# Attention values of a decoder's second layer: full float32 with two heads in the two column halves, in place of split float32 with zero blocks

## The chip, the cores and the metric

The kernel runs on one core of a Trainium2 chip. The metric is the device time of one execution in microseconds (us), taken as the median of several runs. The core has five engines: PE (matmuls; the profile lists its weight loads apart, as PEld), DVE (vector), ACT (scalar), POOL and SP (here it issues the transfers). PE writes its results to PSUM, and DVE and ACT read them from there.

## The reference, cut to what matters

Two decoder layers work on 512 tokens of width 1024. Layer 0 mixes with a gated delta rule beside an attention into 256 memory tokens. Layer 1 mixes with a sliding-window attention of 12 heads (width 64, two shared key/value heads, a sink logit for each head) beside a memory attention of 4 heads. Each mixer is followed by a layer norm, an MLP with a hidden width of 4096, and a layer norm. The change is in the attention of layer 1, of which this is the part that counts:

```python
def mixer_b(h, mem, k_sh, v_sh, cos, sin, w_in, sinks, mem_w_kv, w_o):
    proj = h @ w_in
    q = apply_rope(proj[..., :SWA_Q_W].reshape(B, S, SWA_HEADS, SWA_DH), cos, sin)
    o = sliding_window_sink_attention(q, k_sh, v_sh, sinks)   # o = probs @ values of 2 blocks of 128 keys
    mo = memory_cross_attention(proj[..., SWA_Q_W:], mem, mem_w_kv)   # mo = probs @ 256 memory values
    return jnp.concatenate([o, mo], axis=-1) @ w_o
```

## The kernel before

All arithmetic stands for float32. Most matmuls are done in a faster format on split operands: a number is cut into a high part (ACT casts it) and a low part (DVE subtracts), and three matmuls, high by high, high by low and low by high, make one product. `split_copy` (L117) makes the pair, `token_major` (L106) and `feature_major` (L98) are the products with weights, and `wload` (L81) loads a slab of weights and splits it. A matmul on plain float32 operands stands in the trace as two matmul records.

Layer 1's mixer runs over 4 tiles of 128 tokens (t). `shared_kv` (L1051) makes a tile's rotated keys and its values; `projq` (L1068) makes half of a tile's queries (tile `projqMM`, transposes `projqpt`); `attend` (L1083) pushes two units for each half of a tile, and each unit holds four heads in two pairs (j), with r naming a pair's two heads. In the second half of a tile the second unit is the memory attention (`mem`). So there are 16 units: 12 of the sliding window, 3 of which see one block of keys (t = 0) and 9 two blocks, and 4 of the memory.

A unit has three parts. `scores` (L1097, tile `ssc`) multiplies 64-row operands: the two heads of a pair lie in the two halves of the array's rows, and the softmax follows on DVE (mask and maximum, L1119; scaling, L1137) and ACT (exponential, L1126). `turn` (L1139) transposes the probabilities on PE (tile `spt`, L1145) and copies them out of PSUM. `values` (L1154) multiplies by the values into the tile `ov` and splits the result into `XH`/`XL` or `mixTs`, from which `out1` (L1178) takes it for the output product (`wo`).

In `values` both heads of a pair are summed into one result of 128 rows: head 0 in rows 0 to 63, head 1 in rows 64 to 127. To do that with the array's whole width, the values stand with a block of 64 zeros between the two value heads (`vSs`, `VM1`, L1048 and L1025), and each matmul takes a 128-column slice, values and zeros or zeros and values. Window units work on split probabilities (`pTh`, `pTl`) and split values (`vSh`, `vSl`): 12 matmuls of 256 columns for two blocks, 6 for one. Memory units work in plain float32: 8 matmuls of 128 columns.

`push` (L584) interleaves the units: the scores of the newest, the turn of the one before, the values of the one before that. The order of the steps is the string `LAYER1_ORDER` (L40), run by `run_steps` (L44). On this order the framework's scheduler sets each engine's final order; every engine then works strictly in that order. PSUM tiles rotate: three for the large products (`mm`), five for the small ones (`sm`), and a product waits until the tile three places back has been read.

Of the kernel before, what the change touches and what calls it, by code (L numbers as in the profile page):

```python
# [18 lines left out]
P = 128  # L19
# [30 lines left out]
def trunk(ctx: ExitStack, tc: tile.TileContext, xT, xn, memT, wk, wq, wv, wqm, wz, wmk, wmv, wo0, wo1, up, dn,  # L50
# [533 lines left out]
    def push(unit):  # L584

        unit[0]()
        pend.append(unit)
        if len(pend) > 1:
            pend[-2][1]()
        if len(pend) > 2:  # L590
            pend.pop(0)[2]()
# [428 lines left out]
    with tc.tile_pool(name="l1", bufs=2) as lp:  # L1020
# [3 lines left out]

        KMr, VM1 = lt([P, 2, 256], "pm", 2), lt([P, 2, 2, 3, 64], "VM1", 1)  # L1025
        V.memset(VM1[:, :, :, 1, :], 0.0)
# [3 lines left out]
        for b in range(2):  # L1030
            for j in range(2):
                SY.dma_start(VM1[:, b, j, 0::2, :], kv1[1, :, b * 256 + j * P:b * 256 + (j + 1) * P].rearrange(
                    "p (r d) -> p r d", r=2))
# [14 lines left out]
        vSs = [lt([P, NT, 3, 64], n, 1, F32R) for n in ("vSh", "vSl")]  # L1048
        for v in vSs:
            V.tensor_scalar(v[:, :, 1, :], band[:, :].rearrange("p (t d) -> p t d", t=NT), 0.0, None, op0=ALU.mult)  # L1050
        def shared_kv(t):  # L1051
            ps = mmt("ropeMM")
            token_major(ps[:, :256], slabs["S"], x_tok(XH, t), x_tok(XL, t))
            split_copy(ps[:, P:2 * P].rearrange("p (g d) -> p g d", g=2), *[v[:, t, 0::2, :] for v in vSs])
# [28 lines left out]
        def attend(half, t):  # L1083
# [6 lines left out]
            def unit(q):  # L1090
# [48 lines left out]
                def turn():  # L1139
                    st["pT"] = []  # L1140
                    for r in range(2):
# [4 lines left out]
                        if mem:  # L1146
                            pT = fr(lt([P, 2, 2, P], "pTh", 4, F32R))
                            A.copy(pT, pt)
                        else:
                            pT = [lt([P, 2, 2, P], n, 4, F32R) for n in ("pTh", "pTl")]  # L1150
                            split_copy(pt[:, :nk], *[x[:, :nk] for x in pT])
                        st["pT"].append(pT)

                def values():  # L1154
                    pT = st["pT"]
                    ov = smt("ov")[:, 0:256].rearrange("p (j i) -> p j i", j=2)
                    if mem:
                        for j in range(2):
                            for i in range(4):
                                T.matmul(ov[:, j, :], VM1[:, i % 2, j, i // 2:i // 2 + 2, :].rearrange("p a d -> p (a d)"),  # L1160
                                         pT[i // 2][:, i % 2, j, :], start=(i == 0), stop=(i == 3))
                    else:
                        for r in range(2):
                            ph, pl = pT[r]
                            for b in range(nb):
                                vh, vl = (v[:, t - nb + 1 + b, r:r + 2, :].rearrange("p a d -> p (a d)") for v in vSs)
# [108 lines left out]
```

## Time and profile before

| what | value |
|---|---|
| median of 3 runs | 1191.41 us (1190.02 to 1192.32) |
| the profiled execution's own time | 1191.65 us |
| span of its trace | 1189.9 us |
| granted PE clock, mean | 0.991 |
| PE, DVE, ACT busy, share of the span | 97%, 73%, 48% |
| bytes moved by the transfers | 114.17 MB, 96 GB/s on average |

The profile is of one execution. A row of the trace names the line, the engine, the operation and the tiles (result <- operands); times are in us unless marked ns. In a shape such as 64*128 64x256 the first pair is the part of the array, rows by columns, and the second the operand that is streamed, 64 rows by 256 columns here. Matmul records are pipelined: a record lasts longer than the distance to the next one, so costs are read from start to start. Layer 1's attention lies between about 675 and 810 us of the span.

### The profile page before, as it was taken

The page shows a single profiled execution, that of the slowest core. Times are in us where ns is not written, and L with a number is a line of the kernel's source. Part 1 is how long each engine was busy: PE and PEld are TensorE (multiplying, and loading weights), DVE is VectorE, ACT ScalarE, POOL GpSimd, SP SyncE. Part 2 cuts the span into 40 slices and gives each one's busy share as a digit, 9 for nine tenths or more (in the row PEclk, how much of TensorE's full clock was granted, in tenths as well). Part 3 has the DMA queues.
Part 4 walks back from the last instruction along what each step waited for, and adds up shares of the span by engine and source line. Part 5 has one row for each costly group of instructions (what it writes and reads, how often), then busy time and mean ns, then how long its engine had stood idle before and what let it go on. Part 6 is the DMA issues. An engine that isn't in the chain of part 4 may idle for free.

```text
span 1189.9 us, 19072 instructions
## 1 busy us (share of the span) xinstructions
PE 1158.1 (97%) x7512; PEld 1025.7 (86%) x7512; DVE 866.3 (73%) x1621; ACT 566.3 (48%) x1024; POOL 229.0 (19%) x180
## 2 busy tenths in 40 slices
PE   9899999999999999999999999999999999999996
PEld 8877788879998898998988888788989998989985
DVE  5478889777798666666656968886986666666657
ACT  5345454655484443545443346662653534445341
POOL 0112111101014413232220100000042314232204
PEclk9899999999999999999999999999999999999998
DMA  7522141204324232232424231112333242323311
GB/s 255 176 72 78 60 132 39 67 19 139 130 82 139 79 121 93 90 123 71 141 73 124 72 120 41 38 35 71 107 112 119 74 139 72 128 86 101 112 36 71
DMA packets 41242, 114.17 MB, mean 96 GB/s; under 512 B 12160, under 2 KB 12544, under 8 KB 41152
## 3 DMA queue, kind: packets, MB, share of 16 engines
q1 hardware_dynamic: 40576, 112.04, 28.9%
q8 instruction: 59, 0.97, 0.3%
q10 hardware_dynamic: 576, 0.92, 0.2%
q14 instruction: 31, 0.25, 0.1%
HBM read 109.53 MB, written 3.41 MB: 95 GB/s over the span
## 4 chain that ended last, share of the span: by engine, by line
PE 81%; DVE 11%; ACT 3%; DMA 1%; POOL 1%; issue 1%; POOLq 0%; SPq 0%; ACTq 0%; DVEq 0%
PE dn L113 9%; PE dn L114 9%; PE dn L112 9%; PE upb L866 3%; PE upb L867 3%; PE upb L868 3%; PE wo L113 2%; PE wo L114 2%; PE wo L112 2%; PE upa L867 2%; PE upd L867 2%; PE upa L868 2%; PE upd L868 2%; PE upa L866 2%; PE upd L866 2%; PE up L103 2%
## 5 line engine op out<-in xcount | busy, mean ns | idle before, releaser
L114 PE MATMUL dn<-wh,hl 128*128 128x512 f32 x512 | 200.0, 391 | 0.0
L113 PE MATMUL dn<-wl,hh 128*128 128x512 f32 x512 | 200.0, 391 | 0.0
L112 PE MATMUL dn<-wh,hh 128*128 128x512 f32 x512 | 199.6, 390 | 0.0
L87 ACT CAST wh<-wr 128x1024 fp32r<-128x1024 f32 (+1 forms) x136 | 142.5, 1051 | 103.8 <-PE dn L114 24.8
L88 DVE TENSOR_TENSOR wl<-wr,wh 128x1024 fp32r<-128x1024 f32 (+1 forms) x136 | 166.4, 1225 | 34.1 <-ACT wh L87 31.7
L114 PEld LDWEIGHTS dn<-wh,hl 128*128 128x128 f32 x512 | 96.1, 188 | 20.3
L945 DVE TENSOR_TENSOR res<-res,dn 128x512 f32<-128x512 f32 x120 | 82.0, 683 | 40.7 <-PE dn L114 40.2
L112 PEld LDWEIGHTS dn<-wh,hh 128*128 128x128 f32 x512 | 96.4, 188 | 17.6
L113 PEld LDWEIGHTS dn<-wl,hh 128*128 128x128 f32 x512 | 96.1, 188 | 17.7
L857 POOL TENSOR_TENSOR sa<-wr 128x512 f32<-128x512 f32 x26 | 36.1, 1388 | 370.6 <-DMA wr<-in_up_dram 279.6
L651 POOL TENSOR_TENSOR rs<-rs,nhalf 128x1 f32<-128x1 f32 x16 | 13.3, 834 | 338.1 <-DVE rs L650 282.0
L119 DVE TENSOR_TENSOR wl<-wr,wh 128x1024 fp32r<-128x1024 f32 x26 | 34.1, 1310 | 43.5 <-ACT wh L118 43.5
L118 ACT CAST wh<-sa 128x1024 fp32r<-128x1024 f32 x26 | 27.3, 1050 | 76.6 <-PE upd L867 76.6
L867 PE MATMUL upa<-XL,wh 128*128 128x256 f32 x208 | 58.5, 281 | 0.0
L867 PE MATMUL upd<-XL,wh 128*128 128x256 f32 x208 | 58.5, 281 | 0.0
L868 PE MATMUL upa<-XH,wl 128*128 128x256 f32 x208 | 58.4, 281 | 0.0
L868 PE MATMUL upd<-XH,wl 128*128 128x256 f32 x208 | 58.3, 280 | 0.0
L866 PE MATMUL upa<-XH,wh 128*128 128x256 f32 x208 | 58.3, 280 | 0.0
L866 PE MATMUL upd<-XH,wh 128*128 128x256 f32 x208 | 58.2, 280 | 0.0
L866 PE MATMUL upb<-TH,wh 128*128 128x256 f32 x208 | 58.0, 279 | 0.0
L867 PE MATMUL upb<-TL,wh 128*128 128x256 f32 x208 | 57.8, 278 | 0.0
L868 PE MATMUL upb<-TH,wl 128*128 128x256 f32 x208 | 57.6, 277 | 0.0
(411 smaller groups left out, 3365.7 us busy)
## 6 DMA issues: line engine op xcount, KB each, us to landing
wr<-in_up_dram SPq DMA_DIRECT2D x64, 512.0 KB, 5.4
wr<-in_dn_dram SPq DMA_DIRECT2D x64, 512.0 KB, 4.6
wr<-in_wo_dram SPq DMA_DIRECT2D x16, 512.0 KB, 3.8
wr<-in_bw_dram SPq DMA_DIRECT2D x8, 512.0 KB, 4.3
wr<-in_wz_dram SPq DMA_DIRECT2D x6, 520.0 KB, 4.5
wr<-in_wk_dram SPq DMA_DIRECT2D x6, 512.0 KB, 3.7
wr<-in_wq_dram SPq DMA_DIRECT2D x6, 512.0 KB, 3.5
wr<-in_wv_dram SPq DMA_DIRECT2D x6, 512.0 KB, 3.7
```

The lines of the kernel that those rows point to most:

```text
L87: A.copy(hi, raw)
L88: V.tensor_sub(lo, raw, fr(hi))
L112: T.matmul(ps, sh, hi[:, kk, :], start=(k == 0), stop=False)
L113: T.matmul(ps, sh, lo[:, kk, :], start=False, stop=False)
L114: T.matmul(ps, sl, hi[:, kk, :], start=False, stop=(k == nk - 1))
L118: A.copy(hi, src)
L119: V.tensor_sub(lo, src, fr(hi))
L857: G.tensor_tensor(sa[:, 0], raw[1][:, kA], raw[1][:, kB], op=ALU.add)
L866: T.matmul(ps, hi[:, k, :], mh[:, k, :], start=start and k == 0, stop=False, skip_group_check=True)
L867: T.matmul(ps, hi[:, k, :], ml[:, k, :], start=False, stop=False, skip_group_check=True)
L868: T.matmul(ps, lo[:, k, :], mh[:, k, :], start=False, stop=stop and k == 3, skip_group_check=True)
L945: V.tensor_tensor(dst, dst, ps, op=ALU.add)
```

## The change

The values are kept in plain float32 and without zero blocks (`vS`, `VM1`: two blocks of 64 where there were three). The probabilities are copied out of PSUM unsplit, head r = 0 of each pair by ACT and r = 1 by DVE (`pT`). In `values` every matmul has a stationary operand of 64 columns and writes its own 64 rows of `ov`, so the two heads of a pair lie in the two halves of the array's columns: 4 matmuls of 256 columns for two blocks, 2 for one, and 8 of 128 columns for the memory. `push` gets a flag, set by `attend`, by which the values of the unit two before go ahead of the turn of the unit before, directly behind the scores.

```diff
-    def push(unit):
+    def push(unit, early=False):
         unit[0]()
         pend.append(unit)
+        if early and len(pend) > 2:
+            pend.pop(0)[2]()
         if len(pend) > 1:
             pend[-2][1]()
...
-        KMr, VM1 = lt([P, 2, 256], "pm", 2), lt([P, 2, 2, 3, 64], "VM1", 1)
-        V.memset(VM1[:, :, :, 1, :], 0.0)
+        KMr, VM1 = lt([P, 2, 256], "pm", 2), lt([P, 2, 2, 2, 64], "VM1", 1)
...
-                SY.dma_start(VM1[:, b, j, 0::2, :], kv1[1, :, b * 256 + j * P:b * 256 + (j + 1) * P].rearrange(
+                SY.dma_start(VM1[:, b, j], kv1[1, :, b * 256 + j * P:b * 256 + (j + 1) * P].rearrange(
...
-        vSs = [lt([P, NT, 3, 64], n, 1, F32R) for n in ("vSh", "vSl")]
-        for v in vSs:
-            V.tensor_scalar(v[:, :, 1, :], band[:, :].rearrange("p (t d) -> p t d", t=NT), 0.0, None, op0=ALU.mult)
+        vS = lt([P, NT, 2, 64], "vS", 1)
...
-            split_copy(ps[:, P:2 * P].rearrange("p (g d) -> p g d", g=2), *[v[:, t, 0::2, :] for v in vSs])
+            A.copy(vS[:, t], ps[:, P:2 * P].rearrange("p (g d) -> p g d", g=2))
...
-                        if mem:
-                            pT = fr(lt([P, 2, 2, P], "pTh", 4, F32R))
-                            A.copy(pT, pt)
+                        pT = lt([P, 2, 2, P], "pT", 6)
+                        if r == 0:
+                            A.copy(pT[:, :nk], pt[:, :nk])
                         else:
-                            pT = [lt([P, 2, 2, P], n, 4, F32R) for n in ("pTh", "pTl")]
-                            split_copy(pt[:, :nk], *[x[:, :nk] for x in pT])
+                            V.tensor_copy(pT[:, :nk], pt[:, :nk])
...
-                    if mem:
-                        for j in range(2):
-                            for i in range(4):
-                                T.matmul(ov[:, j, :], VM1[:, i % 2, j, i // 2:i // 2 + 2, :].rearrange("p a d -> p (a d)"),
-                                         pT[i // 2][:, i % 2, j, :], start=(i == 0), stop=(i == 3))
-                    else:
-                        for r in range(2):
-                            ph, pl = pT[r]
-                            for b in range(nb):
-                                vh, vl = (v[:, t - nb + 1 + b, r:r + 2, :].rearrange("p a d -> p (a d)") for v in vSs)
-                                T.matmul(ov, vh, ph[:, b], start=(r == 0 and b == 0), stop=False)
-                                T.matmul(ov, vh, pl[:, b], start=False, stop=False)
-                                T.matmul(ov, vl, ph[:, b], start=False, stop=(r == 1 and b == nb - 1))
+                    for js in (range(0, 1), range(1, 2)) if mem else (range(0, 2),):
+                        js = slice(js[0], js[-1] + 1)
+                        for b in range(nk):
+                            for r in range(2):
+                                v = VM1[:, b, js.start, r, :] if mem else vS[:, t - nb + 1 + b, r, :]
+                                T.matmul(ov[64 * r:64 * r + 64, js, :], v, pT[r][:, b, js, :], start=(b == 0),
+                                         stop=(b == nk - 1))
...
-                push(unit(q))
+                push(unit(q), True)
```

The scheduler's order moves with it. First, PE at the first values of layer 1, before the change: behind the scores of one unit (`ssc_7315`) come the transposes of another (`spt`), then the 12 value matmuls (`ov_7363`; the first three stand here) of a third.

```order
L1110 MATMUL ssc_7315<-kTh_6832,qTl_7163 128x128
L1145 MATMUL spt_7349<-ident,pm_7203 128x128 x4
L1145 MATMUL spt_7356<-ident,pm_7203 128x128 x4
L1167 MATMUL ov_7363<-pTh_7235,vSh_6834 128x256
L1168 MATMUL ov_7363<-pTl_7236,vSh_6834 128x256
L1169 MATMUL ov_7363<-pTh_7235,vSl_6835 128x256
```

The same place after the change: the four value matmuls stand between the scores and the transposes (two of them here, the other two read alike), and one matmul of a query product comes before the next scores.

```order
L1161 MATMUL ov_7337<-pT_7227,vS_6833 64x256
L1161 MATMUL ov_7337<-pT_7234,vS_6833 64x256
L1144 MATMUL spt_7344<-ident,pm_7195 128x128 x4
L1144 MATMUL spt_7351<-ident,pm_7195 128x128 x4
L113 MATMUL projqMM_7408<-wl_7251,XH 128x512
L1109 MATMUL ssc_7358<-KMh_6822,qTh_7154 128x256
```

So whole-array work (transposes, products) no longer stands on both sides of the values: the scores' row halves go straight over into the values' column halves, and these into whole-array work.

Second, PE after the change at the values of the first tile's other unit (`ov_7970`) and, further on, at those of the next tile. Here the scheduler put matmuls of a query product between the two heads of one pair.

```order
L1109 MATMUL ssc_7936<-kTh_6831,qTl_7882 128x256
L1161 MATMUL ov_7970<-pT_7928,vS_6833 64x256
L113 MATMUL projqMM_8101<-wl_7257,XH 128x512
L114 MATMUL projqMM_8101<-wh_7256,XL 128x512
L1161 MATMUL ov_7970<-pT_7933,vS_6833 64x256
L112 MATMUL projqMM_8101<-wh_7256,XH 128x512
```

The two heads of this pair no longer follow each other. The same happens at two more places: one head, two matmuls of the output product, three heads; and three heads, eight matmuls of scores, one head.

Third, DVE at the start of layer 1, before the change: the zero fills (L1050) and the low part of the first values (`vSl`) stand ahead of the split of the last layer norm (L605), and both rotary products on `ropeMM_6864` (L1042, L1043), which are its last readers, behind it.

```order
L709 SCALAR_TENSOR_TENSOR res<-res,rs_6794,lnb_4210 128x512 x2
L1050 TENSOR_SCALAR vSh_6834<-band 128x4x64
L1050 TENSOR_SCALAR vSl_6835<-band 128x4x64
L1065 TENSOR_SCALAR nsink_6846<-sink_b 128x12
L119 TENSOR_TENSOR vSl_6835<-ropeMM_6864,vSh_6834 128x2x64
L605 TENSOR_TENSOR XL<-to_feapt_6799,XH 128x4x128
L605 TENSOR_TENSOR XL<-to_feapt_6808,XH 128x4x128
L1042 TENSOR_TENSOR rp_988_6892<-ropeMM_6864,cosT 128x128
L1043 TENSOR_TENSOR rp_989_6893<-ropeMM_6864,sinT 128x128
```

After the change, on the same engine at the same place (`ropeMM_6860` is now the name of that product):

```order
L1042 TENSOR_TENSOR rp_987_6887<-ropeMM_6860,cosT 128x128
L652 TENSOR_SCALAR rs_6794<-mv_6792 128x1
L710 SCALAR_TENSOR_TENSOR res<-res,mv_6792,lng_4209 128x512 x2
L711 SCALAR_TENSOR_TENSOR res<-res,rs_6794,lnb_4210 128x512 x2
L1043 TENSOR_TENSOR rp_988_6888<-ropeMM_6860,sinT 128x128
L88 TENSOR_TENSOR wl_6937<-wr_6934,wh_6936 128x1024
L607 TENSOR_TENSOR XL<-to_feapt_6799,XH 128x4x128
```

The last reader of the first `ropeMM` tile now comes ahead of the split of the last layer norm, and a weight split (L88) has moved in front of that split.

## The prediction

> **What bounds the kernel now.** I read the page first: span, busy times, and the chain that ended last.
>
> ```profile
> span 1189.9 us, 19072 instructions
> PE 1158.1 (97%) x7512; PEld 1025.7 (86%) x7512; DVE 866.3 (73%) x1621; ACT 566.3 (48%) x1024; POOL 229.0 (19%) x180
> PE 81%; DVE 11%; ACT 3%; DMA 1%; POOL 1%; issue 1%; POOLq 0%; SPq 0%; ACTq 0%; DVEq 0%
> ```
>
> PE sets the time. Whether it does so where the change lies is read from the table of windows, for 700 to 810 us (PE, PEld, DVE, ACT and POOL busy), and from the waits of PE between 680 and 830 us (total, times, longest):
>
> ```profile
> 700.00:810.00 110.00, 105.69 (x726) 87.91 (x725) 88.44 (x307) 65.92 (x206) 0.00 (x0) 1.00 0.12 39
> ```
>
> ```profile
> PE spt L1145 <- DVE pm L1137: 2.7, 2, 1.4
> PE projqpt L1079 <- ACT qr L1076: 1.1, 1, 1.1
> PE ropeMM L112 <- DVE rp L1043: 0.6, 1, 0.6
> PE spt L1145 <- DVE pTl L119: 0.3, 1, 0.3
> ```
>
> PE works 105.69 of 110 us at a full clock (the 1.00), and all its named waits come to 4.7 us. So the change is worth what it takes from PE's own row of work, plus or minus what it does to these few waits. DVE, at 88.44 of 110, is the engine next behind, and the transfers (a share of 0.12) don't matter.
>
> **The values, step by step.** The tile `ov` has these matmuls (durations min/median/max in ns):
>
> ```profile
> L1160 PE MATMUL ov<-pTh,VM x64: 275/275/275, 725.2 to 757.4; 128*128 128x128 f32 x64
> L1167 PE MATMUL ov<-pTh,vSh x42: 276/280/387, 719.1 to 805.0; 128*128 128x256 f32 x42
> L1168 PE MATMUL ov<-pTl,vSh x42: 276/280/365, 719.3 to 805.1; 128*128 128x256 f32 x42
> L1169 PE MATMUL ov<-pTh,vSl x42: 276/279/285, 719.5 to 805.3; 128*128 128x256 f32 x42
> ```
>
> The durations overlap, so I take distances between starts, from PE's timeline:
>
> ```profile
> 719.33 0.28 PE L1168 MATMUL ov<-pTl,vSh 128*128 128x256 f32 x1
> ...
> 720.51 0.28 PE L1169 MATMUL ov<-pTh,vSl 128*128 128x256 f32 x1
> 720.72 0.39 PE L1110 MATMUL ssc<-KMh,qTh 64*128 64x256 f32 x2
> 720.95 0.28 PE L1110 MATMUL ssc<-KMl,qTh 64*128 64x256 f32 x2
> ...
> 721.42 0.28 PE L1110 MATMUL ssc<-KMh,qTl 64*128 64x256 f32 x2
> 721.63 0.50 PE L113 MATMUL projqMM<-wl,XH 128*128 128x512 f32 x1
> 721.97 0.39 PE L114 MATMUL projqMM<-wh,XL 128*128 128x512 f32 x1
> 722.20 0.40 PE L112 MATMUL projqMM<-wh,XH 128*128 128x512 f32 x1
> ...
> 725.20 1.95 PE L1160 MATMUL ov<-pTh,VM 128*128 128x128 f32 x16
> ```
>
> From the second to the twelfth value matmul of a unit are ten steps in 1.18 us: 0.118 each. The 126 split matmuls cost 126 x 0.118 = 14.9 us. The memory's 16 records (8 matmuls, two records each) end after 1.95 us, the last one lasting 0.275, so their step is 1.675/15 = 0.112; 64 of them cost 7.2 us. **Values before: 22.1 us.**
>
> After the change 42 plain float32 matmuls of 256 columns and 32 of 128 remain, two records each. A record of plain float32 takes 0.112 for 128 columns, so about 0.22 for 256. What isn't in the trace is two of them side by side in column halves. The nearest rows have the same format, side by side in row halves: layer 0's memory scores, from the timeline and from the list of tile `msc`.
>
> ```profile
> 163.00 1.13 PE L542 MATMUL msc<-KM,res 64*128 64x256 f32 x8
> ```
>
> ```profile
> L542 PE MATMUL msc<-KM,res x32: 376/376/480, 163.0 to 207.4; 64*128 64x256 f32 x32
> ```
>
> Eight records end after 1.13 us; less the last one's 0.376 their starts lie within 0.754. One after another they would need seven steps of 0.22, 1.54 us. As four pairs they have three steps, the first 0.104 longer (480 against 376): (0.754 - 0.104)/3 = 0.217. So two halves cost what one costs. The `ssc` rows above say the same of the split format: x2 every 0.118.
>
> If column halves do as row halves do, the values cost 42 x 0.217 = 9.1 (21 pairs, two steps each) plus 32 x 0.112 = 3.6, together 12.7: **-9.4 us**. The bound from the other side is no overlap at all: 84 x 0.217 + 64 x 0.112 = 25.4, which is +3.3. I take the first, since the row halves stand in the same array with the same format.
>
> Three pairs are torn apart by the new order (one head, other work, the other head). Each loses one overlap, 2 x 0.217: **+1.3**.
>
> **The changes of array form.** From the last `ov` at 720.51 to the second projection at 721.97 PE goes from the whole array to row halves and back: 1.46 us, where one step of 0.118, six pairs of 0.118 and one projection of 0.23 would be 1.06. So two changes of form cost 0.40, one 0.20. In the order of layer 1's mixer I count 38 changes before and 58 after, since values between scores and transposes add one each, and the torn pairs more. 20 x 0.20 = **+4.0**. From row halves to column halves isn't in the trace. Between nothing (both are halves) and 0.20 I take 0.20; there are 16 such places, so nothing would be 3.2 less.
>
> **DVE and ACT.** They lose work, from the lists of tiles `spt` and `mpt` (layer 0's copy, the form that DVE now does):
>
> ```profile
> L118 ACT CAST pTh<-spt x24: 372/584/617, 714.9 to 802.6; 128x512 fp32r<-128x512 f32 x18, 128x256 fp32r<-128x256 f32 x6
> L119 DVE TENSOR_TENSOR pTl<-spt,pTh x24: 418/683/693, 716.2 to 803.6; 128x512 fp32r<-128x512 f32 x18, 128x256 fp32r<-128x256 f32 x6
> L1148 ACT COPY pTh<-spt x8: 586/590/594, 718.7 to 751.7; 128x512 f32<-128x512 f32 x8
> ```
>
> ```profile
> L566 DVE COPY pT<-mpt x4: 674/682/692, 178.5 to 225.9; 128x512 f32<-128x512 f32 x4
> ```
>
> ACT goes from 32 copies to 16, DVE from 24 subtractions to 16 copies of the same length. Neither sets the end, so this alone is worth nothing; it counts where PE waits for them.
>
> At 682 us (0.6 of the waits) a key product waits for DVE to read the PSUM tile three places back. Ahead of that reader stood the layer norm's split:
>
> ```profile
> 680.39 1.29 DVE L605 TENSOR_TENSOR XL<-to_feapt,XH 128x512 fp32r<-128x512 f32 x2 [0.16 <-ACT XH L604]
> ```
>
> Now the reader stands ahead of it, and these 1.29 us are more than the wait. **-0.6**, with bounds 0 and -0.6. A weight split has come in front of the layer norm's split there, but what needs that split on PE is the fourth key product, behind two others of some 2.8 us each (24 steps of 0.118).
>
> At 717 us (1.1) ACT's copy for `projqpt` stood behind two probability copies and a weight cast:
>
> ```profile
> 714.88 1.07 ACT L118 CAST pTh<-spt 128x512 fp32r<-128x512 f32 x2
> 715.84 1.06 ACT L87 CAST wh<-wr 128x1024 fp32r<-128x1024 f32 x1
> 716.79 0.39 ACT L1076 COPY qr<-projqMM 128x256 f32<-128x256 f32 x1
> ```
>
> The cast keeps its place and one of the two copies goes: 0.5 less. At 752 us, in one of the two waits for scaled probabilities (2.7 together), two copies stood ahead of the exponentials in the same way:
>
> ```profile
> 751.18 1.08 ACT L1148 COPY pTh<-spt 128x512 f32<-128x512 f32 x2 [1.08 <-PE spt L1145]
> 752.22 0.40 ACT L1126 ACTIVATE pm<-pm,smx 128x128 f32<-128x128 f32 x1
> ```
>
> In ACT's new order there the exponentials come first and the one copy left behind them: 1.0 less for the probabilities, though the next values then wait for that copy (below). At both waits the values also fill PE's time between scores and transposes (0.9 us for a memory unit, 8 steps of 0.112). Of the 2.7 I take 1.9 off. The 0.3 for `pTl` goes with that subtraction.
>
> Together -2.7. Against it stands a new wait: values follow the next unit's scores, so the copies of `spt` must come through while these scores run, 0.91 us (720.72 to 721.63) for a copy of 0.68 on DVE that may still be reducing. What is queued behind such a wait is all of PE's work. The nearest row is PE's 0.3 for `pTl`. At the places with no product in between I reckon four such waits, the one at 752 us among them: +1.2. Net **-1.5**, with bounds -3.5 (all of the 4.1 that isn't the first wait's, less half of the new ones) and +0.5.
>
> The other edits cost nothing: the four transfers to `VM1` keep their place and size, and the zero fills leave DVE ahead of the place just told.
>
> A rule speaks against the change. The Trainium skill, page "TensorE: Matmul & The Clock Gate", section "Part 3: Packing small matmuls — row/col tiling", says that weight loads overlap with matmuls in flight only where the row groups differ, and the two column halves share all rows. The trace disagrees with a strict reading: the loads of the memory scores,
>
> ```profile
> 163.00 0.73 PEld L542 LDWEIGHTS msc<-KM,res 64*128 64x128 f32 x8
> ```
>
> are all done 0.73 us after the first, by when the starts of the matmuls have only just ended (0.754), so each half's next load went in while its own rows were working. No run here shows it for columns.
>
> **The sum.** -9.4 + 1.3 + 4.0 - 0.6 - 1.5 = -6.2 us. The profiled execution's own time is 1191.65 (span 1189.9 and 1.75 around it), so 1185.5. It stands 0.24 above the median of the runs, 1191.41, which is within their spread of 2.3; I leave it. The forecast's own range is 1182.5 to 1188.5: the row-to-column change at nothing (-3.2) at one end; the waits at their worst (+2.0) and changes of form 0.05 dearer at the other.
>
> **The rivals.**
>
> *The column halves don't overlap* (slower). Each pair's four records run one behind the other, as the 16 memory records do now. Place: all 16 value blocks. Price: +3.3 in place of -9.4, no loss for torn pairs, the same changes of form and waits: +3.3 + 4.0 - 2.1 = +5.2, 1196.9. It decides where less than about 46% of the full overlap is reached (5.2 of 5.2 + 6.2). For it: no row has column halves on the same rows. Against: `msc` and `ssc`. Chance 0.14.
>
> *Loads exposed* (the rule above as a mechanism): the halves compute side by side, but each step first waits for its weights. A first record after a change of form shows an exposed load as 0.104 (480 against 376 ns). 74 steps x 0.104 = 7.7: -6.2 + 7.7 = +1.5, 1193.2. Chance 0.12.
>
> *The waits eat it*: the copies come late at 12 of the 16 values (12 x 0.3 = 3.6 in place of 1.2), and the old waits stay (+2.7): -6.2 + 2.4 + 2.7 = -1.1, 1190.5. For it: DVE at 80%. Against: both engines lose work. Chance 0.14.
>
> **How the numbers follow.** About 0.2% of the time, 2.4 us, is what a measurement of this kernel tells from no change: faster is below 1189.0, slower above 1193.8. The forecast has 0.56, and 0.04 remains for what I haven't seen, half on each side. Faster: 0.56, 0.02 and 0.02 of the waits' case, 0.60. Same: 0.12 of the waits, 0.10 of the loads, 0.22. Slower: 0.14, 0.02 and 0.02 of the loads, 0.18. The range goes from 1182.5 to 1193.5: it takes in the forecast, the waits and most of the loads (0.8) and leaves out the halves that don't overlap.
>
> **What would show it.** In the profile after: `ov` records as 128*64, coming in pairs at a step near 0.217 (256 columns) and 0.112 (128) where the pair is whole; a step of 0.43 for a pair's two records each would be the first rival, one of 0.32 and 0.22 the second. Some 0.1 on each side of a value block for the changes of form. PE's wait at `ropeMM` gone; waits for `pm` below 1 us in all; PE waiting at `ov` for `pT` no more than four times and 0.3 each. A value block with a wait of 0.5 or more at most places would make the prediction wrong through the third rival.

## The result and the profile after

| | before | after |
|---|---|---|
| median of the runs, same chip | 1191.87 us (1190.02 to 1192.34, 4 runs) | 1182.97 us (1179.73 to 1183.56, 4 runs) |
| profiled execution | 1191.65 us, span 1189.9 | 1183.56 us, span 1181.8 |

The ratio is 0.9923, with a 95% interval of 0.9901 to 0.9944: 0.8% faster, and 2.5 us below the forecast of 1185.5. The page's head for the kernel after, with the shares of the chain that ended last:

```profile
span 1181.8 us, 18955 instructions
PE 1153.5 (98%) x7470; PEld 1013.4 (86%) x7470; DVE 857.4 (73%) x1606; ACT 559.3 (47%) x1008; POOL 220.7 (19%) x180
PE 83%; DVE 10%; ACT 3%; DMA 1%; POOL 1%; issue 1%; POOLq 0%; SPq 0%; ACTq 0%; DVEq 0%
```

PE still sets the time; it is busy 4.6 us less (1158.1 to 1153.5), and the span is 8.1 shorter. So over half of the gain is work that PE no longer has, and the rest is waiting that has gone.

Where that happened is read by landmarks. The first `ropeMM` record starts at 670.96 us before and at 671.27 after, so up to there the two executions are alike. From there to the first `projqMM` 0.8 goes (14.31 to 13.56), and to the first `up` of layer 1 another 7.4; behind it 0.2. The stretch from the first `projqMM` to the first `up` of layer 1 is called the stage below, and each kernel is judged by its row of the table of windows: from where to where, length, then busy time and count of PE, PEld, DVE, ACT and POOL, granted clock, DMA share and GB/s. Length less PE's busy time is what PE waited. The row of before:

```profile
685.27:840.98 155.71, 151.41 (x944) 125.25 (x942) 122.27 (x373) 79.83 (x226) 2.77 (x3) 1.00 0.17 58
```

and that of after:

```profile
684.83:833.10 148.27, 146.19 (x902) 112.26 (x900) 116.52 (x362) 72.80 (x210) 2.77 (x3) 1.00 0.18 60
```

PE's work in the stage fell by 5.2 us and its waiting from 4.3 to 2.1. The waits of PE after, from 675 to 830 us (total, times, longest):

```profile
PE ov L1161 <- ACT pT L1147: 0.8, 1, 0.8
PE projqpt L1078 <- ACT qr L1075: 0.8, 1, 0.8
PE spt L1144 <- DVE smx L1118: 0.4, 1, 0.4
```

Both waits for scaled probabilities (2.7), the one for `pTl` (0.3) and the one at `ropeMM` (0.6) are gone; two new ones have come (0.8 and 0.4).

The tile `ov` after, weight loads and matmuls:

```profile
L1161 PEld LDWEIGHTS ov<-pT,vS x84: 132/136/137, 717.2 to 796.7; 128*64 128x64 f32 x84
L1161 PE MATMUL ov<-pT,vS x84: 379/379/430, 717.2 to 796.9; 128*64 128x256 f32 x84
L1161 PEld LDWEIGHTS ov<-pT,VM x64: 132/137/137, 721.0 to 752.0; 128*64 128x64 f32 x64
L1161 PE MATMUL ov<-pT,VM x64: 272/273/324, 721.0 to 752.1; 128*64 128x128 f32 x64
```

All have the shape 128*64: half of the array's columns. PE's timeline shows what that takes:

```profile
717.03 0.28 PE L1109 MATMUL ssc<-kTh,qTl 64*128 64x128 f32 x2
717.23 1.08 PE L1161 MATMUL ov<-pT,vS 128*64 128x256 f32 x8
718.25 0.66 PE L1144 MATMUL spt<-ident,pm 128*128 128x128 f32 x4
719.28 0.66 PE L1144 MATMUL spt<-ident,pm 128*128 128x128 f32 x4 [0.38 <-DVE smx L1118]
...
721.02 1.09 PE L1161 MATMUL ov<-pT,VM 128*64 128x128 f32 x16
```

Eight records of 256 columns, the two matmuls (two records each) of each head, begin and end within 1.08 us, and sixteen of 128 columns within 1.09. The eight records start in pairs at 717.231 and .238, .498 and .505, .714 and .721, .930 and .936: a step of 0.216, which serves both heads. In the memory blocks the step is 0.109. From the last score to the first value record (717.03 to 717.23) it is 0.20, where 0.11 is the scores' own step: 0.09 for the change of array form. The first step of the block is 0.267 in place of 0.216, so 0.05 at most for the first load.

The step of 0.109 is shorter than one load (136 to 137 ns), and two loads go in during it. The Trainium skill, page "TensorE: Matmul & The Clock Gate", section "Part 3: Packing small matmuls — row/col tiling", has loads overlap matmuls in flight only where the row groups differ. Here both halves use all rows and the loads are hidden, so the trace disagrees.

Three blocks are torn by a projection, as foreseen. One of them:

```profile
764.60 0.65 PE L1161 MATMUL ov<-pT,vS 128*64 128x256 f32 x2
765.18 0.50 PE L113 MATMUL projqMM<-wl,XH 128*128 128x512 f32 x1
765.51 0.40 PE L114 MATMUL projqMM<-wh,XL 128*128 128x512 f32 x1
765.84 0.65 PE L1161 MATMUL ov<-pT,vS 128*64 128x256 f32 x2
```

Each head takes 0.65 here by itself, as long as a block of the same size that isn't torn takes for both.

Summed from start to start over the stage's records, against the steps within one form, the 7.4 us come from: the values, 22.9 us before and 14.3 after with their torn pairs, -8.6; the changes of array form, 38 before and 58 after in PE's order, 5.9 and 10.0 us, +4.2; the waits, -2.2; and a remainder of -0.8 in the steps of whole-array matmuls, which nothing here explains. The split depends on where the first steps behind a transpose or a change of form are booked. By steps alone the values are 21.8 before (126 x 0.118 + 64 x 0.109) and 12.5 after (84 x 0.108 + 64 x 0.0545), with 1.3 for the torn pairs and 0.6 for two blocks that get their second head late, told below: -7.4. With the first step behind each change counted to it in both kernels, the changes are 6.9 and 10.0, +3.1. So about 1 us can move between the terms.

### The profile page after: what moved, and what is told of

Same layout as the page of the kernel before. It is cut to its first block, busy times and chain, and to the rows that moved or that the text cites. A ratio compares the mean times of both kernels' runs of the same rounds, so it can differ in the third digit from the quotient of the medians.

```text
span 1181.8 us, 18955 instructions
## 1 busy us (share of the span) xinstructions
PE 1153.5 (98%) x7470; PEld 1013.4 (86%) x7470; DVE 857.4 (73%) x1606; ACT 559.3 (47%) x1008; POOL 220.7 (19%) x180
## 3 DMA queue, kind: packets, MB, share of 16 engines
HBM read 109.53 MB, written 3.41 MB: 96 GB/s over the span
## 4 chain that ended last, share of the span: by engine, by line
PE 83%; DVE 10%; ACT 3%; DMA 1%; POOL 1%; issue 1%; POOLq 0%; SPq 0%; ACTq 0%; DVEq 0%
PE dn L113 9%; PE dn L114 9%; PE dn L112 9%; PE upb L868 3%; PE upb L869 3%; PE upb L870 3%; PE wo L114 2%; PE wo L112 2%; PE wo L113 2%; PE upa L869 2%; PE upd L869 2%; PE upa L870 2%; PE upd L870 2%; PE upa L868 2%; PE upd L868 2%; PE up L103 2%
## 5 line engine op out<-in xcount | busy, mean ns | idle before, releaser
L88 DVE TENSOR_TENSOR wl<-wr,wh 128x1024 fp32r<-128x1024 f32 (+1 forms) x136 | 166.4, 1226 | 34.1 <-ACT wh L87 31.7
L859 POOL TENSOR_TENSOR sa<-wr 128x512 f32<-128x512 f32 x26 | 39.2, 1506 | 373.8 <-DMA wr<-in_up_dram 306.2
```

The source lines that it names most:

```text
L88: V.tensor_sub(lo, raw, fr(hi))
L859: G.tensor_tensor(sa[:, 0], raw[1][:, kA], raw[1][:, kB], op=ALU.add)
```

## The experiments

The theory is that of the prediction: the two column halves compute at the same time, a change of form costs about 0.2, a torn pair the whole of the shorter half, and the early place changes waits by a little. The rivals are told with each run. The first question is which part of the change the gain belongs to, the second whether PE's side of it is understood. The time of an execution up to layer 1's attention differs by up to 5.6 us among kernels whose layer 0 is the same (the first `ropeMM` starts between 666.1 and 671.7 us), and it did by 3.5 between two profiles of the kernel after. So the stage's row is given beside each time.

In these rows the granted clock has to be read first. In four of the runs below it is under 1.00, because for one or two stretches of 3.41 us inside the stage PE was granted half of its clock. These are the two of the run with new values late:

```profile
753.33:756.74 3.41, 3.41 (x24) 2.65 (x24) 1.63 (x13) 2.22 (x11) 0.00 (x0) 0.50 0.03 5
766.98:770.39 3.41, 3.32 (x15) 1.94 (x15) 1.88 (x5) 0.37 (x1) 0.00 (x0) 0.50 0.80 292
```

In such a stretch a step takes about twice its time. A memory block, 1.09 in the kernel after, takes

```profile
754.09 1.98 PE L1161 MATMUL ov<-pT,VM 128*64 128x128 f32 x16
```

So each stretch adds up to 1.7 us, half of its length, to PE's work in the row. The others begin at 770.87 (full float32 with zeros), 768.96 (second head first, twice) and 766.11 (two units at a time). All five begin within 2 us of the end of a wait of PE of 1.5 to 2.3 us, and in the stages that have no such stretch no wait of PE is longer than 1.43. But one wait of 1.8, with new values late, has none behind it, so it is likely and not shown that the long waits bring them.

**Heads apart.** All matmuls of one head of a block before those of the other:

```diff
-                    for js in (range(0, 1), range(1, 2)) if mem else (range(0, 2),):
-                        js = slice(js[0], js[-1] + 1)
-                        for b in range(nk):
-                            for r in range(2):
+                    for r in range(2):
+                        for js in (range(0, 1), range(1, 2)) if mem else (range(0, 2),):
+                            js = slice(js[0], js[-1] + 1)
+                            for b in range(nk):
```

> The changed kernel, but in the values all matmuls of one head of a pair come before all of the other, so that the two column halves can overlap at most at the seam; number, size and format of the matmuls, and everything on ACT and DVE, stay. Theory (the gain is PE time: the two halves compute side by side): a window unit with two blocks then takes three steps of a matmul (0.43 us each) instead of two, +0.43 for 9 units; a memory unit seven steps of 0.218 instead of four, +0.65 for 4; units with one block stay. +3.9 + 2.6 = +6.5 us over the changed kernel, less 0.4 to 0.9 as the order tears only two pairs instead of three: about +5.5 to +6 us. Rival (the gain is what ACT and DVE no longer do, and PE would wait for them anyway): 0 to +2 us.

Measured: 1185.9 us (1185.08 to 1186.23, 6 runs), ratio to before 0.996 (0.9947 to 0.9973).

```profile
685.28:835.83 150.55, 148.46 (x901) 114.90 (x900) 116.79 (x362) 72.89 (x210) 2.77 (x3) 1.00 0.18 59
```

The stage is 2.3 longer than after, all of it PE's own work; the waiting is the same 2.1. The first window block and the first memory block on the timeline:

```profile
717.70 1.09 PE L1161 MATMUL ov<-pT,vS 128*64 128x256 f32 x8
...
721.47 1.58 PE L1161 MATMUL ov<-pT,VM 128*64 128x128 f32 x16
```

The memory block grew from 1.09 to 1.58, but the window block stayed at 1.09. The single records say why: in the window block they still start in pairs (717.695 and .708, .962 and .975). The order of PE's queue is head 0, head 0, head 1, head 1, and yet a record of head 1 begins 13 ns after the first of head 0, ahead of three records of head 0 that stand in front of it. In the memory block, where eight records of head 0 come first, five start alone (721.471, .631, .740, .849, .958) and only then the other head's (.964), again with three of head 0 still to start. So the memory part of the theory held, and its window part fell: PE takes a matmul for the free column half past waiting ones of the other half, three records of them in both places. The same section of the Trainium skill's page has matmuls start strictly in their order; this trace disagrees. So what the section on the kernel before says, that every engine works strictly in its order, doesn't hold on PE between the two halves.

**Blocks by head.** To test that reading, the same reordering within one pair of heads only, so that no more than three records ever have to be passed:

```diff
                         for b in range(nk):
-                            for r in range(2):
...
+                        for r in range(2):
+                            for b in range(nk):
```

> The kernel after, with the two matmuls of one head ahead of the two of the other within each token pair, in memory units and window units alike (in the kernel after the heads alternate). Theory (PE lets a matmul for the free column half pass as many as three waiting records of the other half, as the memory units with the heads apart showed: the other head began with three records of the first left): nothing is lost, a memory block takes 0.05 + 8 x 0.109 = 0.92 us from its first start to its last start and step; with 56 changes of form in place of 58 and two blocks torn in place of three the stage takes 148.3 - 0.4 - 0.4 = 147.5 us. Rival (the passing belongs to the longer records of 256 columns): the four memory blocks run in series, 1.8 us each, +3.5, the stage at 151.

Measured: 1184.45 us (1182.01 to 1186.08, 6 runs), ratio 0.9954 (0.9938 to 0.997).

```profile
721.67 1.14 PE L1161 MATMUL ov<-pT,VM 128*64 128x128 f32 x16
...
772.54 2.17 PE L1161 MATMUL ov<-pT,vS 128*64 128x256 f32 x8
...
783.59 1.08 PE L1161 MATMUL ov<-pT,vS 128*64 128x256 f32 x4
...
785.27 1.08 PE L1161 MATMUL ov<-pT,vS 128*64 128x256 f32 x4
```

The memory block takes 1.14, next to the 1.09 of alternating heads and far from the 1.8 of the rival: the passing of three records holds for the short ones too. But the forecast for the stage (147.5) failed; it took 149.73. Two window blocks show it: one torn between its heads, which now costs all four steps of a head (1.08 and 1.08 in place of one 1.08), and one that ran in series without being torn (2.17 at 772.54; with the heads apart it does the same). The weight loads show why PE passed nothing in that block:

```profile
773.64 0.62 PEld L1161 LDWEIGHTS ov<-pT,vS 128*64 128x64 f32 x4 [0.47 <-DVE pT L1149]
```

These are the second head's. DVE's copy for it, queued behind a weight split, runs only from 772.90 to 773.58, and head 0's last record starts at 773.24. So head 0 was through before the other head had its operand. It is the block that the kernel after has torn between the first record pair of head 0 and the rest. Another 0.5 is a wait at `ropept` that the kernel after doesn't have.

**Full float32 with zeros.** The kernel before, with its blocks of zeros and the old place of the values, but window units on plain float32 and unsplit copies, one on each engine:

```diff
-                        if mem:
-                            pT = fr(lt([P, 2, 2, P], "pTh", 4, F32R))
-                            A.copy(pT, pt)
+                        pT = lt([P, 2, 2, P], "pT", 6)
+                        if r == 0:
+                            A.copy(pT[:, :nk], pt[:, :nk])
                         else:
-                            pT = [lt([P, 2, 2, P], n, 4, F32R) for n in ("pTh", "pTl")]
-                            split_copy(pt[:, :nk], *[x[:, :nk] for x in pT])
+                            V.tensor_copy(pT[:, :nk], pt[:, :nk])
...
-                                vh, vl = (v[:, t - nb + 1 + b, r:r + 2, :].rearrange("p a d -> p (a d)") for v in vSs)
-                                T.matmul(ov, vh, ph[:, b], start=(r == 0 and b == 0), stop=False)
-                                T.matmul(ov, vh, pl[:, b], start=False, stop=False)
-                                T.matmul(ov, vl, ph[:, b], start=False, stop=(r == 1 and b == nb - 1))
+                                v = vS[:, t - nb + 1 + b, r:r + 2, :].rearrange("p a d -> p (a d)")
+                                T.matmul(ov, v, pT[r][:, b], start=(r == 0 and b == 0), stop=(r == 1 and b == nb - 1))
```

> The kernel before, with the window units in plain float32 and probabilities copied out unsplit (one head by ACT, one by DVE), but with the zero blocks, 128 columns and the old place of the values: the relief of ACT and DVE without the column halves. Theory: PE's values cost 1.72 instead of 1.41 us in 9 units and 0.86 instead of 0.71 in 3, +3.3 us; four changes of array form fewer, -0.8; the waits of PE for ACT and DVE shrink by some 2 to 3 us as they did in the changed kernel: about 0 against the kernel before (-1 to +1). Rival (relief of ACT and DVE is the gain): -5 to -8 us against the kernel before.

Measured: 1190.1 us (1187.41 to 1194.29, 12 runs), ratio 1.0004 (0.999 to 1.0017): no difference in time.

```profile
680.13:838.97 158.84, 154.88 (x902) 125.30 (x900) 118.84 (x363) 72.50 (x210) 2.77 (x3) 0.99 0.17 57
```

The same eight records that take 1.08 us in column halves are here

```profile
713.78 1.99 PE L1164 MATMUL ov<-pT,vS 128*128 128x256 f32 x8
```

so the halves save 0.91 of 1.99. PE's work rose by 3.5 us against before. Up to 1.7 of that is the stretch at half clock, which leaves some 1.8 where the theory had 2.5 (3.3 - 0.8). The waits are the other finding:

```profile
PE spt L1144 <- DVE pm L1136: 2.9, 2, 1.9
PE projqpt L1078 <- ACT qr L1075: 0.8, 1, 0.8
```

With half of the copies and all of the subtractions gone, PE waits for scaled probabilities as long as before (2.9 against 2.7). Lifting work off ACT and DVE took only 0.3 from `projqpt` and the 0.3 of `pTl`.

**Old values early.** The kernel before, with the flag of `push` set and nothing else:

```diff
+        if early and len(pend) > 2:
+            pend.pop(0)[2]()
...
-                push(unit(q))
+                push(unit(q), True)
```

> The kernel before with the values placed directly behind the scores, and nothing else. Theory: no work of PE changes, the array form changes as often as before (38); only the waits for the scaled probabilities (2.7 us) can shrink since the values now fill time ahead of the transposes, and new waits for the split copies can come: -2 to +1 us against the kernel before. Rival (the new place is most of the gain): -4 us or more.

Measured: 1191.4 us (1187.61 to 1193.93, 12 runs), ratio 1.001 (0.9997 to 1.0023).

```profile
683.79:840.56 156.77, 152.58 (x944) 126.00 (x942) 122.20 (x373) 79.45 (x226) 2.77 (x3) 1.00 0.17 57
```

```profile
PE ov L1170 <- DVE pTl L119: 1.0, 1, 1.0
PE ov L1162 <- ACT pTh L1150: 0.9, 1, 0.9
...
PE spt L1147 <- DVE pm L1139: 0.2, 1, 0.2
```

The waits for `pm` fall from 2.7 to 0.2, and new ones come for the split copies, which now have less time: 4.2 in all, as before. PE's work, which the theory left as it was, grew by 1.2, and what lengthened it isn't shown. The place alone gains nothing.

**New values late.** The kernel after without the flag:

```diff
-                push(unit(q), True)
+                push(unit(q))
```

> The changed kernel with the values in the old place, behind the transposes of the unit before. The order on PE changes the array form 58 times as in the changed kernel, and tears two pairs instead of three. Theory: PE's work is the same less 0.4 us; waits for the scaled probabilities come back in part, 0.5 to 2.5 us: 0 to +2 us against the changed kernel. Rival (the new place is most of the gain): +4 us or more.

Measured: 1189.19 us (1184.49 to 1191.37, 12 runs), ratio 0.9984 (0.9969 to 0.9999).

```profile
683.94:839.73 155.79, 148.17 (x901) 113.06 (x900) 117.39 (x362) 73.28 (x210) 2.77 (x3) 0.98 0.17 57
```

```profile
PE spt L1144 <- DVE pm L1136: 3.3, 2, 1.8
PE projqpt L1078 <- DVE qr L1045: 1.8, 1, 1.8
...
```

Here the theory fell, and the rival's time came. The stage is as long as before the change (155.8 against 155.7): PE works 3.2 us less than before and waits 3.3 more. But PE's 148.2 hold the two stretches at half clock. Less the 3.4 us that these can have added it is 144.8, an estimate, 6.6 below the kernel before. So the new values do take work from PE at the old place; half of that goes into waits, and the other half is lost to the clock. Shorter values leave less between one unit's scores and its transposes, and the softmax doesn't get faster. The twelve times agree: four executions at granted clocks of 0.992 to 0.994 took 1184.5 to 1186.0 us, where the kernel before, run beside them, took 1187.1 to 1192.3 at these clocks; the other eight, at 0.986 to 0.990, took 1188.3 to 1191.4. The four runs make a table of the stage and of PE's waiting in it:

| | old place | early place |
|---|---|---|
| old values | 155.7, waits 4.3 | 156.8, waits 4.2 |
| new values | 155.8, waits 7.6, two stretches at half clock | 148.3, waits 2.1 |

In the length of the stage each edit alone is worth nothing; together they are worth 7.4 us. That isn't because the new values save nothing by themselves: what they save at the old place is spent on waits and on the clock. The early place puts the values where the softmax needs cover, and with it no wait above 0.8 is left that half clock might follow. The unsplit copies, one step where a split takes a cast and a subtraction behind it, let the values come that early: the old values wait 1.9 us there for their split copies. Unsplit copies with zero blocks at the early place were not run, so how much of the low waits is owed to the copies alone isn't shown.

**Copies on one engine.** To see whether it also takes two engines: both copies on ACT.

```diff
-                            V.tensor_copy(pT[:, :nk], pt[:, :nk])
+                            A.copy(pT[:, :nk], pt[:, :nk])
```

> The kernel after, with both copies of the transposed probabilities on ACT (one each on ACT and DVE in the kernel after). In PE's order 52 changes of array form in place of 58 and two blocks torn in place of three. Theory (the early place lives on copies that run at the same time): the second copy lands some 0.58 us later at each of 16 units, and the scores in between run only 0.9 to 1.1 us, so the values wait: PE's waits in the stage grow from 2.08 us to 5 or more, against -1.2 - 0.4 for the changes and the torn block: the stage at 149.5 to 152 us. Rival (the copies need not run side by side; what bought the waits was only the lifted load on the two engines): waits below 3, the stage at 146.5 to 148.

Measured: 1181.82 us (1178.5 to 1185.28, 6 runs), ratio 0.994 (0.992 to 0.9961).

```profile
683.78:833.61 149.83, 145.23 (x902) 111.60 (x900) 109.83 (x346) 79.16 (x226) 2.77 (x3) 1.00 0.18 58
```

```profile
PE wo L112 <- ACT XH L118: 1.3, 1, 1.3
PE ropept L1058 <- DVE kr L1045: 1.2, 1, 1.2
PE projqpt L1078 <- ACT qr L1075: 1.1, 1, 1.1
PE ov L1161 <- ACT pT L1147: 0.9, 1, 0.9
```

The stage falls into the theory's range (149.5 to 152) and the waits, 4.6, between the two. But the reason given was wrong: the values wait for a copy at one place (0.9, and 0.8 after), not at most of the 16. What grew is what else stands in ACT's queue, `qr` and `XH`, and the 1.2 for `kr` at `ropept`, a wait that is left open below. So by this run it isn't the copies standing side by side that lets the values come early at most places, but what the copies leave of the engine that makes them. The time isn't told apart from that of after.

**Second head first.** In each pair the head whose copy DVE makes goes first:

```diff
-                            for r in range(2):
+                            for r in (1, 0):
                                 v = VM1[:, b, js.start, r, :] if mem else vS[:, t - nb + 1 + b, r, :]
```

> The kernel after, with the second head's value matmul issued ahead of the first head's in each pair. In PE's order no value block is torn by a projection any more (the kernel after has three torn, 1.3 us by the prediction's price) and the changes of array form go from 58 to 60. Theory (a torn pair costs the whole shorter column half, a change 0.2): the stage from the first projqMM to the first layer-1 up takes 148.3 - 1.3 + 0.4 = 147.4 us, the time about 0.9 below the kernel after, ratio near 0.9915 to the kernel before. Rival (PE fills the free half from further back on its queue, as with the heads apart, so a torn pair costs little): stage 148.3 + 0.4 = 148.7.

Measured: 1179.38 us (1177.44 to 1182.28, 6 runs), ratio 0.9919 (0.9901 to 0.9937). It was run again beside the kernel after:

> The second head's value matmul first in each pair, once more and beside the kernel after on the same chip. If the torn blocks are what it saves: stage 146.7 us again, the time 0.9 to 1.6 below the kernel after. Rival (the order of two matmuls changes nothing that a measurement tells, and the 1.6 us were one execution's): stages within 0.3 of each other.

> The kernel after once more, beside the next run. Stage 148.3 us again if it repeats to 0.3; it tells how far a difference of 1.6 us in that stage can be trusted.

Measured: second head first 1179.94 us (1178.07 to 1181.88, 6 runs), ratio 0.9919 (0.9901 to 0.9937); after 1180.41 (1179.78 to 1183.26, 6 runs), ratio 0.9929 (0.9912 to 0.9945). The stage of the kernel after, again:

```profile
681.28:829.45 148.17, 146.09 (x901) 112.26 (x900) 116.47 (x362) 72.78 (x210) 2.77 (x3) 1.00 0.18 58
```

of the second head first, in its first run:

```profile
683.74:830.43 146.69, 144.82 (x901) 111.19 (x900) 116.91 (x362) 72.53 (x210) 2.77 (x3) 1.00 0.18 59
```

and in its second:

```profile
682.91:830.40 147.49, 145.01 (x901) 111.07 (x900) 116.83 (x362) 72.51 (x210) 2.77 (x3) 1.00 0.18 61
```

The stage of after repeats to 0.1. Between the two second runs it differs by 0.7, where the theory had 146.7 once more, 1.5 less than the 148.17 beside it, and the rival less than 0.3. With the second head first PE works 1.1 to 1.4 us less, and every window block of two key blocks is one row of 1.08; close to the 0.9 that the theory gave for the torn pairs less two more changes of form. The waits differ between its two runs by 0.6, a wait at `ropept` that the first didn't have. The times of the two kernels, 1179.9 and 1180.4 on one chip, aren't told apart. A second source of the saved work shows at one memory block, which after takes

```profile
740.63 1.38 PE L1161 MATMUL ov<-pT,VM 128*64 128x128 f32 x16
```

and, with the second head first, 1.09. After, DVE's copy for it runs from 740.18 to 740.87, and the second head's records begin only at 740.929: a late copy that no list of waits shows, since the first head kept PE busy meanwhile. A window block of the kernel after is late in the same way (1.39 in place of 1.08 at 747.27, with DVE's copy ending at 747.53), and with the second head first it takes 1.08. Against that, one memory block there waits for ACT's copy, 1.85 from start to end in the first run.

**Second head first, twice.** The transposes and copies in that order as well:

```diff
-                    st["pT"] = []
-                    for r in range(2):
+                    st["pT"] = [None, None]
+                    for r in (1, 0):
                         pt = smt("spt").rearrange("p (b j i) -> p b j i", b=2, j=2)
...
-                        st["pT"].append(pT)
+                        st["pT"][r] = pT
...
-                            for r in range(2):
+                            for r in (1, 0):
```

> As the run before, and the transposes and copies of the second head also come first. In PE's order 53 changes of array form in place of 58, and one value block torn in place of three (after its first record). Theory (0.2 a change, 0.43 a torn pair, waits as they are): -1.0 - 0.9 = -1.9, the stage at 146.4 us. Rival (the changes of form are cheap and the order of the copies sets the waits): the stage stays at 148 or grows with PE's waits, which are 2.08 us in the kernel after.

Measured: 1184.4 us (1180.38 to 1186.4, 8 runs), ratio 0.9955 (0.994 to 0.9969).

```profile
679.65:832.09 152.44, 146.00 (x902) 112.33 (x900) 117.10 (x362) 72.28 (x210) 2.77 (x3) 0.99 0.17 58
```

```profile
PE wo L112 <- ACT XH L118: 2.3, 1, 2.3
PE ssc L1109 <- ACT qTh L118: 0.8, 1, 0.8
...
```

The theory (146.4) failed, and it failed in the waits. PE's work went down by only 0.2, but a stretch at half clock lies in it; less the 1.7 us which that can have added, it went down by about the 1.9 that were foreseen. The waits went from 2.1 to 6.4: the order of the copies moves ACT's and DVE's other work, and waits spring up at `wo` and `ssc` where there were none. The rival had this right.

**Two units at a time.** Both units of a half pushed as one, with one more pair of buffers for what then lives longer:

```diff
-            for q in range(2):
-                push(unit(q), True)
+            two = [unit(q) for q in range(2)]
+            push([lambda i=i: [u[i]() for u in two] for i in range(3)], True)
```

> The kernel after, with the two units of a half of the heads pushed as one: the scores of both stand together, then the transposes of both, then the values of both. In PE's order 34 changes of array form in place of 58, and no block torn in place of three. Theory (a change costs 0.2 us, each): -24 x 0.2 - 1.3 = -6.1 at most, less whatever new waits for softmax and copies come; with the waits unchanged the stage takes 142.2 us. If the changes in the middle of a stream cost less than 0.1, -3.7 at most. Rival (the distance between scores and transposes, and between copies and values, is what the early place bought; in larger lumps it is lost at the ends of each lump): waits grow from 2.1 to 6 us or more and eat the gain, the stage at 148 or above.

Measured: 1189.39 us (1184.11 to 1192.0, 12 runs), ratio 0.9992 (0.9976 to 1.0008).

```profile
680.38:833.64 153.26, 144.16 (x902) 112.97 (x900) 115.76 (x362) 71.34 (x210) 2.77 (x3) 0.99 0.18 58
```

```profile
PE ssc L1109 <- ACT pT L1147: 1.9, 1, 1.9
PE projqpt L1078 <- DVE qr L1045: 1.2, 1, 1.2
PE spt L1144 <- DVE mixl L119: 1.1, 1, 1.1
```

The rival held: with 34 changes of form in place of 58 the waits rise from 2.1 to 9.1, and the gain is lost. The profiled execution, 1184.1 us at a granted clock of 0.994, is the shortest of the twelve; ten of the others have 0.984 to 0.989 and take 1187.4 to 1192.0. So the median pays for more than this row shows, and the clock goes with it. The price of a change is confirmed on the way: summed as above, changes cost 10.0 us after and 5.5 here, 4.5 for 24 of them, 0.19 each; with the first steps booked to them in both kernels it is 0.16. PE's work fell by 2.0 in all, because score and whole-array steps became longer by 3.0 together. Of that some 1.1 is the stretch at half clock, whose first 2.2 us fall on scores; what lengthened the rest isn't shown.

## Why the prediction was right

*The column halves overlap.* Right, and with it the first rival falls: steps of 0.216 and 0.109 for both heads where 0.217 and 0.112 were foreseen. The loads are hidden but for 0.05 at most at the start of a block, so the second rival falls too (74 steps of 0.104 would have been 7.7 us).

*Values and torn pairs* were to bring -9.4 + 1.3 = -8.1 and brought -8.6, or -7.4 by steps alone. The run with the second head first shows the torn blocks to be about that dear: PE works 1.1 to 1.4 less without them, though with two more changes, without the two blocks that waited for DVE's copy, and with one that waits for ACT's.

*Changes of form* were priced at +4.0 and cost +4.2, or +3.1, by how their first steps are booked.

*The waits* were the mis-sized term: -0.6 at `ropeMM` and -1.5 for the rest were foreseen; -0.6 came at the first and -2.2 at the others. The wait at 752 us came where it was foreseen, but as one of 0.8; of the four waits of 0.3 for copies no other came. And of the 2.7 for scaled probabilities all went, not 1.9.

Here a step of the reasoning failed, though its sum came out near. The prediction put these waits down first to ACT's queue (one copy fewer ahead of the exponentials) and only then to the values that fill PE's time. The run with unsplit copies and the old place keeps 2.9 of them, and the one with old values at the early place 0.2: it is the place alone that removes them. And the prediction had no row for what the new values would do at the old place, 7.6 us of waits and two stretches at half clock. It treated two edits as terms to be added; in the length of the stage each alone is worth nothing. That the term for the waits came near is in part luck: the relief of the two engines, on which it leans, is worth 0.6 by the run with zeros.

*Not foreseen* was the remainder of -0.8 us. And the lower end of the forecast's own range, 1185.5 - 3.2, is 1182.3 and not 1182.5; the measured median lies above both.

The third rival, that waits eat the gain, fell for this change; but it is what happened to the new values at the old place, with both copies in the other order, and with two units at a time, each time with half clock behind the waits.

## What to carry to other kernels

Work taken from the bounding engine in the middle of a chain is also cover taken from that chain: ask what waited behind it unseen, and move the shortened work to where the cover is short before judging it. Where two edits meet in one chain, measure both alone and both together; a sum of their single effects can miss the whole gain. Where PE's busy time grows without more work, look at the granted clock of that stretch before anything else. And a list of waits shows only an idle engine: a half-used array, as with a torn or late pair, counts as busy, and is found by a block that takes longer than its twins.

## What the runs showed of the hardware

- Two matmuls in the two column halves, on the same rows and with different weights, run at the same time: 1.08 us for eight float32 records of 256 columns, against 1.99 for the same count over all columns.
- PE starts a matmul for the free column half ahead of waiting ones for the busy half, past three records and not past more in the blocks seen here. Strict order between halves can't be relied on for timing. Passing needs the other half's operand to be there: one block of eight records ran in series (2.17 us) because its second head's copy came late.
- A change of array form costs 0.16 to 0.19 us, as a mean over 24 of them.
- In four of the stages PE was granted half of its clock (0.50) for stretches of 3.41 us, five in all, and a memory block takes 1.98 us there in place of 1.09. Each stretch began within 2 us of the end of a wait of 1.5 to 2.3 us; stages without a wait above 1.43 had none.
- Left open: a wait of 0.5 to 1.2 us at `ropept` for DVE's `kr` that comes in some executions and not in others, of the same kernel too (none and 0.6).
